# Weight sums of three FFN column blocks made during the softmax stage, and a reordered end of the down stage, in a hybrid decoder layer

## The chip, the cores and the metric

The kernel runs on one core of a Trainium2 chip. That core has five engines that work through their own instruction lists in order and wait for each other on semaphores: PE (TensorE, matrix products), DVE (VectorE), ACT (ScalarE), POOL (GpSimd) and SP (SyncE, which issues all DMAs here). The metric is the time of one execution on the device in microseconds (us).

## The reference

One decoder layer on a sequence of 1024 rows of width 1024, all in fp32. The middle (attention) is left out here; the parts that the change touches are the feed-forward network (FFN) and the last LayerNorm.

```python
mod = (c @ w_c + b_c).reshape(B, 6, D)              # shift, scale, gate for mixer and FFN
u = x * (1.0 + scale_m) + shift_m
proj = u @ w_in                                     # split into FoX and GLA parts
y = concat([fox_attention(...), gla_attention(...)]) @ w_o   # softmax heads, gated linear attention
x = layer_norm(ALPHA * x + (1.0 + gate_m) * y, ln1_g, ln1_b)
u2 = x * (1.0 + scale_f) + shift_f
h = silu(u2 @ w_gate) * (u2 @ w_up)                 # D_FF = 2816
y2 = h @ w_down
x = layer_norm(ALPHA * x + (1.0 + gate_f) * y2, ln2_g, ln2_b)
```

## The kernel before, in words

Every fp32 operand of a product is split into a high and a low part (`split`: a cast on ACT, L87, and a subtraction on DVE, L88), and each product is three matmuls (high x high, high x low, low x high). A matmul writes 128 rows x 512 columns of a PSUM bank. A scheduler decides the order of each engine's list when the kernel is built, from the order of the code and a few `after` and `issue_after` marks.

The program passes through these stages: modulation and projections, gated linear attention, the softmax heads (about 378 to 570 us of the profile below), the mixer's output with the first LayerNorm (to about 606), the FFN loop (to about 1050) and the down stage (to the end).

**The softmax heads.** Sixteen steps, four for each of four pairs of heads. `fox_load` brings the q and k rows of the next pair into four tiles named `stk` (loads of k_d and q_d, L748), in two column ranges. These tiles are the ones that the last scores of the pair before read, so their loads wait for these scores. `fox_scores` makes scores `sc` (PE, L766 and L767), an exponential (DVE L771, ACT L775, DVE L778, POOL L779, tile `pr`), and `fox_values` transposes `pr` (PE `tr`, L795) and multiplies with the values (PE `pv`, L807). Rows of the output projection (`yg`, `xbuf`, `rp_d`) fill in between.

**The FFN loop.** D_FF is cut into 22 column blocks of 128. For each, the gate and the up product of 1024 rows are made as one 2x2 block product with seven products in place of eight (Winograd's form). It needs sums of weights and sums of activations: `sum_weights(f, g, u, w)` splits B22 (the second half of up), makes T1 to T4 in place with four DVE operations (L1014 to L1017), and splits both tiles into `hi` and `lo`. `first_weights` splits the gate block itself (B11, B21). The activation sums S1 to S4 and A22 are made once by `second_operands` (DVE L972 for the sums, L88 and L87 for the splits, tiles `s` and `a`). A block's products run in `group_parts`; `first()` is the order of block 0 (T3, T1, T4, T2, B22). Tiles of a weight kind (`wtile("raw" / "hi" / "lo")`) have three buffers each, so a fourth one waits until all readers of the first have run.

**The mixer units** before the loop (`late`, tiles `r`): 12 matmuls `yo` for each of two halves of 512 columns and four row groups, then DVE adds the bank to the row (L894), and statistics and normalization follow. A unit's bank comes free with that addition. Two banks are in turn.

**The sums for the down stage.** `w_sums(i)`, called 11 times inside the loop, makes sums of two row blocks of w_down in place (tiles `wd`) and stores them to DRAM (`t_d`, two stores of 512 KB); `h_sums` does so for the activations h (`a_d`).

**The down stage.** Again seven products, each of six groups of two pieces of 128 contraction rows (one piece in the last group); `group` loads one group of both sides and splits it; `mms` issues its matmuls `dn` (L1213) for the four row groups q. Three products end with the banks being read to `dc` and added to the result rows: `add_rows` (multiply by the gate L1230, add L1231, statistics), then `out_norm` (L1307: subtract the mean, times l2g; L1314 or ACT L1311 with POOL L1312: times the deviation, plus l2b; two stores of 512 columns each). The last product, a_cols(1, 1) with t_rows(1, 0), goes onto the banks `sa` of the product before it; groups 2 to 5 are kept in SBUF, and the matmuls then go row group by row group, so that each row group's normalization follows while the next is multiplied.

SP issues the DMAs in the order of its list. Eight semaphores go round: a DMA waits until the one that used its semaphore before has landed.

## Time and profile before

| | |
|---|---|
| median of 3 runs | 1282.32 us (1281.34 to 1286.94) |
| the profiled execution | 1279.93 us, of which the span of the trace is 1278.1 |
| granted TensorE clock | 0.989 of full speed, mean |
| busy PE / DVE / ACT / POOL | 1222.8 / 794.4 / 514.3 / 225.2 us |
| DMA | 209.65 MB, 164 GB/s over the span |

Busy is the time in which an engine had an instruction in work; the rest of the span it waited. The granted clock tells how fast TensorE was let run; at 1.00 it is on the higher of its two levels (2.4 GHz), and a stretch well below 1.00 holds time on the lower one (1.2 GHz).

### The profile page before, as it was taken

To read this page: it belongs to the slowest core of one execution; us is meant where nothing else is said; L and a number is where in the kernel's file an instruction comes from. 1 tells how busy PE (TensorE), PEld (TensorE's weight loads), DVE (VectorE), ACT (ScalarE), POOL (GpSimd) and SP (SyncE) were. 2 spreads that over 40 slices of the span, in tenths; PEclk is the share of its full clock that TensorE was granted. 3 is DMA by queue.
4 is the path that set the end of the run, shared out by engine and by line. 5 is a ranking of instruction groups with operands and counts; after the bars stand their busy time and mean duration, and the time that the engine had idled before them with its cause. 6 is when DMAs were issued, how large, how long until landed. Compare 5 with 4: busy or idle time off the path is not lost.

```text
span 1278.1 us, 16493 instructions
## 1 busy us (share of the span) xinstructions
PE 1222.8 (96%) x6177; PEld 991.8 (78%) x6177; DVE 794.4 (62%) x1180; ACT 514.3 (40%) x876; POOL 225.2 (18%) x204
## 2 busy tenths in 40 slices
PE   6999999999999999999889999999999999999986
PEld 4889997899777767667768888888888887887875
DVE  7656529631554434548875665765765668585697
ACT  3422346422354466664623333333332344344341
POOL 3500032420233324322000000000000024060014
PEclk9999999999999999999989999999999999999999
DMA  9865625311465446133363454444444358675561
GB/s 298 258 221 189 202 65 173 108 42 40 137 196 162 145 126 202 67 133 112 102 214 131 142 180 173 173 161 144 174 166 162 125 206 287 223 238 189 196 232 66
DMA packets 144442, 209.65 MB, mean 164 GB/s; under 512 B 8100, under 2 KB 90406, under 8 KB 144364
## 3 DMA queue, kind: packets, MB, share of 16 engines
q1 hardware_dynamic: 144364, 208.62, 49.7%
q8 instruction: 48, 0.79, 0.2%
q14 instruction: 30, 0.25, 0.1%
HBM read 153.65 MB, written 54.94 MB: 163 GB/s over the span
## 4 chain that ended last, share of the span: by engine, by line
PE 75%; DVE 8%; DMA 7%; ACT 3%; POOL 3%; issue 3%; SPq 1%; POOLq 0%; DVEq 0%; ACTq 0%
PE ga L1028 18%; PE dn L1213 15%; PE gc L1028 9%; PE pv L807 4%; PE gb L1028 4%; DMA wc<-in_w_c_dram 4%; PE tr L795 3%; PE acc L330 2%; PE acc L332 2%; PE acc L331 2%; PE sc L767 1%; PE sc L766 1%; PE at L516 1%; DVE lo L88 1%; PE yg L717 1%
## 5 line engine op out<-in xcount | busy, mean ns | idle before, releaser
L88 DVE TENSOR_TENSOR lo<-raw,hi 128x1024 fp32r<-128x1024 f32 (+1 forms) x112 | 150.2, 1342 | 98.9 <-ACT hi L87 94.7
L87 ACT CAST hi<-raw 128x1024 fp32r<-128x1024 f32 (+1 forms) x112 | 114.7, 1026 | 123.3 <-PE ga L1028 44.5
L1028 PE MATMUL ga<-s,hi 128*128 128x512 f32 x344 | 109.0, 397 | 7.8 <-ACT hi L87 7.0
L1213 PE MATMUL dn<-hi,ah 128*128 128x512 f32 x280 | 111.7, 400 | 4.0 <-DVE dc L1287 3.5
L1213 PE MATMUL dn<-lo,ah 128*128 128x512 f32 x280 | 111.4, 398 | 2.5 <-DVE lo L88 2.4
L1213 PE MATMUL dn<-hi,al 128*128 128x512 f32 x280 | 110.4, 396 | 0.0
L1246 POOL TENSOR_TENSOR r<-r,l1g 128x1024 f32<-128x1024 f32 x8 | 23.3, 2920 | 491.1 <-DMA r<-z_d 490.0
L330 PE MATMUL acc<-hi,uh 128*128 128x264 f32 (+1 forms) x384 | 108.7, 284 | 0.5 <-ACT m L531 0.5
L332 PE MATMUL acc<-hi,ul 128*128 128x264 f32 (+1 forms) x384 | 108.7, 284 | 0.0
L331 PE MATMUL acc<-lo,uh 128*128 128x264 f32 (+1 forms) x384 | 108.7, 283 | 0.0
L88 DVE TENSOR_TENSOR al<-ar,ah 128x1024 fp32r<-128x1024 f32 (+1 forms) x38 | 54.5, 1436 | 49.6 <-ACT ah L87 49.3
L1028 PEld LDWEIGHTS ga<-s,hi 128*128 128x128 f32 x344 | 65.6, 191 | 24.0 <-ACT hi L87 7.5
L87 ACT CAST ah<-ar 128x1024 fp32r<-128x1024 f32 (+1 forms) x38 | 37.3, 984 | 101.7 <-PE dn L1213 95.8
L771 DVE CUSTOM_DVE_ANT_0 pr<-sc,smask 128x128 f32<-128x128 f32 (+7 forms) x64 | 47.8, 756 | 44.1 <-PE tr L795 19.2
L330 PEld LDWEIGHTS acc<-hi,uh 128*128 128x128 f32 x384 | 72.8, 190 | 1.6 <-issue 0.8
L331 PEld LDWEIGHTS acc<-lo,uh 128*128 128x128 f32 x384 | 72.8, 190 | 0.6 <-issue 0.2
L332 PEld LDWEIGHTS acc<-hi,ul 128*128 128x128 f32 x384 | 72.7, 190 | 0.4 <-issue 0.2
L1028 PE MATMUL ga<-s,lo 128*128 128x512 f32 x172 | 68.7, 400 | 0.0
L1213 PEld LDWEIGHTS dn<-hi,ah 128*128 128x128 f32 x280 | 53.4, 191 | 17.2 <-issue 3.9
L779 POOL TENSOR_SCALAR pr<-pr,sm 128x128 f32<-128x128 f32 (+7 forms) x64 | 48.5, 762 | 98.6 <-DVE sm L778 74.8
L1213 PEld LDWEIGHTS dn<-lo,ah 128*128 128x128 f32 x280 | 53.3, 190 | 15.4 <-DVE lo L88 3.3
L801 ACT COPY pt<-tr 128x512 f32<-128x512 f32 (+1 forms) x80 | 43.0, 542 | 53.3 <-PE tr L795 52.2
(347 smaller groups left out, 2924.0 us busy)
## 6 DMA issues: line engine op xcount, KB each, us to landing
ar<-a_d SPq DMA_DIRECT2D x35, 512.0 KB
wc<-in_w_c_dram SPq DMA_DIRECT2D x32, 512.0 KB
raw<-in_w_gate_dram SPq DMA_DIRECT2D x25, 512.0 KB
wd<-in_w_down_dram SPq DMA_DIRECT2D x22, 512.0 KB
t_d<-wd SPq DMA_DIRECT2D x22, 512.0 KB
a_d<-hf SPq DMA_DIRECT2D x22, 512.0 KB
u<-in_w_up_dram SPq DMA_DIRECT2D x21, 512.0 KB
raw<-t_d SPq DMA_DIRECT2D x20, 512.0 KB
```

The lines of the kernel that those rows point to most:

```text
L87: nc.scalar.copy(dst_hi, src)
L88: return nc.vector.tensor_tensor(dst_lo, src, dst_hi.bitcast(F32), op=ALU.subtract).ins
L330: nc.tensor.matmul(ps, uh[k][:, ts], wh[:, k % 4, :], start=k == 0, stop=False)
L331: nc.tensor.matmul(ps, uh[k][:, ts], wl[:, k % 4, :], start=False, stop=False)
L332: nc.tensor.matmul(ps, ul[k][:, ts], wh[:, k % 4, :], start=False, stop=k == NK - 1)
L771: nc.vector.tensor_tensor_reduce(t[:, 0:nk], sc[:, 0:nk], smask[:, S - nk : S], op0=ALU.add, op1=ALU.min, scale=-1.0, scalar=3e38, accum_o ...
L779: nc.gpsimd.tensor_scalar(t[:, 0:nk], t[:, 0:nk], sm[:, 2:3], 1.0, op0=ALU.mult, op1=ALU.mult)
L795: nc.tensor.transpose(tr[:, m * P : (m + 1) * P], ps_[2 * j + par][:, (2 * kk + a) * P : (2 * kk + a + 1) * P], ident,)
L801: nc.scalar.copy(pt[:, par, 0:w], tr[:, 0:w])
L807: nc.tensor.matmul(pv[64 * par : 64 * par + 64, q0:256], fv_t(kb)[:, 64 * h : 64 * h + 64], pt[:, par, a * 256 : a * 256 + 256 - q0], star ...
L1028: ins = nc.tensor.matmul(ps, x, y, start=start and j == 0 and i == 0, stop=j == NJ - 1 and i == 2, skip_group_check=not start,)
L1213: last["dn"] = nc.tensor.matmul(ps, x[:, a, qs], y[:, a, :], start=start and a == 0 and i == 0, stop=stop and a == n - 1 and i == 2, skip_ ...
```

## The change

Three things change, and two small ones with them. (1) For blocks 0, 1 and 2 of the FFN the sums T1 to T4 and B22 are made during the softmax heads (`pre_sums`, in the order 1, 2, 0; 9 pieces over the first seven steps, by the table `PRE`) and stored, already split, to DRAM: five tiles of 512 KB per block, `p_d`. At the FFN's start `load_sums` loads them, and `sum_weights` is no longer called for these blocks. (2) `w_sums` also splits its T4 part and stores the two parts (`t4_d`). The last product of the down stage loads them in place of loading and splitting. (3) At the end of the down stage the reads of the four banks come ahead of the fourth `out_norm` of the first half and of the `add_rows` of the second, and row group 3 is multiplied in two column ranges of 256. The last normalization of row group 2 moves from ACT and POOL to DVE, behind that of row group 3.

```diff
+    def pre_sums(f):
+        def load():
+            for n, i, src in (("g", 28, w_gate), ("u", 29, w_up)):
+                t = s_[n] = slot(i, (NK, P), name="pw")
+                nc.sync.dma_start(t, src[:, f * P : (f + 1) * P].rearrange("(k p) n -> p k n", p=P))
+        def sums():
+            b = slot(30, (2, NJ, P), dt=F32R, name="pb")
+            split(b[:, 0], b[:, 1], u[:, NJ:NK])
+            nc.sync.dma_start(p_d[f][0], b.rearrange("p a k n -> p (a k n)").bitcast(F32))
+            weight_sums(g, u)
+        def parts():
+            for k, (n, t) in enumerate((
+                ("u", slot(31, (NK, P), dt=F32R, name="ph")),
+                ("g", cp.tile([P, NK, P], F32R, tag="c4a", name=nm("ph"))),
+            )):
+                raw = s_[n]
+                split(t, raw.bitcast(F32R), raw)
+                nc.sync.dma_start(p_d[f][1 + 2 * k], t.rearrange("p k n -> p (k n)").bitcast(F32))
+                nc.sync.dma_start(p_d[f][2 + 2 * k], raw.rearrange("p k n -> p (k n)"))
+        return [load, sums, parts]
...
-    def load_up(f):
-        u = wtile("raw", (NK, P), F32) if f == 0 else slot((4, 5)[f % 2], (NK, P), name="u")
+        u = slot((4, 5)[f % 2], (NK, P), name="u")
...
+    def load_sums(f, w):
+        t14 = wtile("hi", (NK, P), F32R), wtile("lo", (NK, P), F32R)
+        if f == 1:
+            t32 = [slot(i, (NK, P), dt=F32R, name="t32") for i in (4, 5)]
+        else:
+            t32 = wtile("hi", (NK, P), F32R), wtile("lo", (NK, P), F32R)
+        b = slot((3, 25)[f % 2], (2, NJ, P), dt=F32R, name="b22")
+        for k, t in ((1, t32[0]), (2, t32[1]), (3, t14[0]), (4, t14[1])):
+            nc.sync.dma_start(t.rearrange("p k n -> p (k n)").bitcast(F32), p_d[f][k])
+        nc.sync.dma_start(b.rearrange("p a k n -> p (a k n)").bitcast(F32), p_d[f][0])
...
     def w_sums(i):
...
-        for k, w in enumerate((w0, w1)):
-            nc.sync.dma_start(t_d[i // 2][i % 2, k, :, :], w.rearrange("p a n -> p (a n)"))
+        t4h = cp.tile([P, 512], F32R, tag="m1", name=nm("t4h"))
+        t4l = w1[:, 0, :].bitcast(F32R)
+        split(t4h, t4l, w1[:, 0, :])
+        nc.sync.dma_start(t_d[i // 2][i % 2, 0, :, :], w0.rearrange("p a n -> p (a n)"))
+        nc.sync.dma_start(t_d[i // 2][i % 2, 1, :, 512:1024], w1[:, 1, :])
+        nc.sync.dma_start(t4_d[i // 2][i % 2, 0, :, :], t4h.bitcast(F32))
+        nc.sync.dma_start(t4_d[i // 2][i % 2, 1, :, :], w1[:, 0, :])
...
             split(ah, al, raw)
-            split(bh, bl, braw)
+            if bsrc is not None:
+                split(bh, bl, braw)
+            else:
+                for k, t in enumerate((bh, bl)):
+                    nc.sync.dma_start(t.bitcast(F32), t4_d[m][0:n, k, :, :].rearrange("i p n -> p i n"))
...
-            out_norm(0, q, ra[q], bsa[q], l2g, l2b)
+            if q < 3:
+                out_norm(0, q, ra[q], bsa[q], l2g, l2b)
         product(sa, a_cols(2, 1), t_rows(0, 1), False)
...
         for q in range(4):
-            nc.vector.tensor_tensor(c5[q], sa[q], c5[q], op=ALU.add)
-            add_rows(rb, bsb, q, 1, c5[q])
-        asrc, bsrc = a_cols(1, 1), t_rows(1, 0)
+            c22 = nc.vector.tensor_tensor(c5[q], sa[q], c5[q], op=ALU.add).ins
+        asrc = a_cols(1, 1)
         for m in range(2):
-            g = group(m, asrc, bsrc)
+            g = group(m, asrc, None)
             for q in range(4):
                 mms(sa[q], q, g, False, False, False)
-        kept = [group(m, asrc, bsrc, True) for m in range(2, NG)]
+        with tc.issue_after(c22):
+            out_norm(0, 3, ra[3], bsa[3], l2g, l2b)
+            kept = [group(m, asrc, None, True) for m in range(2, NG)]
+            for q in range(4):
+                add_rows(rb, bsb, q, 1, c5[q])
         for q in range(4):
-            for g in kept:
-                mms(sa[q], q, g, False, g is kept[-1], False)
             t = slot(30, (512,), name="tmp") if q % 2 else tmpb
...
+            for cs in (slice(0, 512),) if q < 3 else (slice(0, 256), slice(256, 512)):
+                for g in kept:
+                    mms(sa[q], q, g, False, g is kept[-1], False, cs)
+                nc.vector.tensor_tensor(t[:, cs], sa[q][:, cs], gf[:, cs], op=ALU.mult)
+                nc.vector.tensor_tensor(rb[q][:, cs], rb[q][:, cs], t[:, cs], op=ALU.add)
...
+            if q != 2:
+                end = out_norm(1, q, rb[q], bsb[q], l2g, l2b)
+            else:
+                m2 = first_norm(rb[q], bsb[q], l2g)[0]
+        with tc.issue_after(end):
+            last_norm(1, 2, rb[2], m2, l2b)
...
+    PRE = (1, 2, 1, 1, 2, 1, 1) + (0,) * 9
...
+        for _ in range(PRE[idx]):
+            pre.pop(0)()
...
-    g = load_gate(0)
-    sum_weights(0, g, load_up(0), ws[0])
+    load_sums(0, ws[0])
```

Three places in the lists show how the instructions move (line numbers are those of the file in question; a trailing number tells tiles of one name apart).

SP, in the softmax stage, at the loads of the second pair of heads. Before:

```order
167 L700 DMA rp_d<-xbuf 128x512
168 L694 DMA xbuf<-in_x_dram 128x512
169 L700 DMA rp_d<-xbuf 128x512
170 L694 DMA xbuf<-in_x_dram 128x512
171 L748 DMA stk_3058<-k_d_1800 128x256
172 L748 DMA stk_3060<-k_d_1800 66x256
173 L748 DMA stk_3057<-q_d_1796 128x768
174 L748 DMA stk_3058<-k_d_1800 128x768
```

And now, with `pw` the raw gate and up blocks and `p_d` the stored sums:

```order
172 L843 DMA p_d_3_3065<-ph_3663 128x1024
173 L844 DMA p_d_2_3064<-pw_3557 128x1024
174 L694 DMA xbuf<-in_x_dram 128x512
175 L844 DMA p_d_4_3066<-pw_3555 128x1024
176 L700 DMA rp_d<-xbuf 128x512
177 L827 DMA pw_3769<-in_w_up_dram 128x8x128
178 L827 DMA pw_3767<-in_w_gate_dram 128x8x128
179 L694 DMA xbuf<-in_x_dram 128x512
180 L748 DMA stk_3073<-k_d_1800 128x256
181 L748 DMA stk_3075<-k_d_1800 66x256
182 L748 DMA stk_3072<-q_d_1796 128x768
183 L748 DMA stk_3073<-k_d_1800 128x768
```

The loads `stk` stand behind stores of sums and loads of the next block's weights, where before only rows of the output projection stood.

PE, in block 0 of the FFN, from T2 (tile `s` 971 to 974 before, 983 to 986 now, is S2) to the next block's first product. Before:

```order
3014 L1028 MATMUL ga_5633<-s_972_5808,hi_5549 128x512 x2
3015 L1028 MATMUL ga_5633<-s_972_5808,lo_5550 128x512
3016 L1028 MATMUL ga_5633<-s_973_5811,hi_5549 128x512 x2
3017 L1028 MATMUL ga_5633<-s_973_5811,lo_5550 128x512
3018 L1028 MATMUL ga_5633<-s_974_5814,hi_5549 128x512 x2
3019 L1028 MATMUL ga_5633<-s_974_5814,lo_5550 128x512
3020 L1028 MATMUL gc_5848<-s_975_5821,b_928_5542 128x512 x3
3021 L1028 MATMUL gc_5848<-s_976_5824,b_928_5542 128x512 x3
3022 L1028 MATMUL gc_5848<-s_977_5827,b_928_5542 128x512 x3
3023 L1028 MATMUL gc_5848<-s_978_5830,b_928_5542 128x512 x3
3024 L1028 MATMUL ga_5676<-s_971_5805,hi_5919 128x512 x2
```

And now (`hi_5627` and `lo_5628` are block 0's T3 and T2, `hi_6070` and `lo_6071` are block 2's):

```order
3009 L1079 MATMUL gc_5924<-s_978_5862,lo_5626 128x512
3010 L1079 MATMUL ga_5709<-s_983_5881,hi_5627 128x512 x2
3011 L1079 MATMUL ga_5709<-s_983_5881,lo_5628 128x512
3012 L1079 MATMUL ga_5709<-s_984_5884,hi_5627 128x512 x2
3013 L1079 MATMUL ga_5709<-s_984_5884,lo_5628 128x512
3014 L1079 MATMUL ga_5709<-s_985_5887,hi_5627 128x512
3015 L1079 MATMUL ga_5807<-s_983_5881,hi_6070 128x512 x2
3016 L1079 MATMUL ga_5709<-s_985_5887,hi_5627 128x512
3017 L1079 MATMUL ga_5709<-s_985_5887,lo_5628 128x512
3018 L1079 MATMUL ga_5709<-s_986_5890,hi_5627 128x512 x2
3019 L1079 MATMUL ga_5709<-s_986_5890,lo_5628 128x512
3020 L1079 MATMUL ga_5807<-s_983_5881,lo_6071 128x512
```

The first matmuls with block 2's T2 have moved into block 0's T2. The loads of `hi_6070` and `lo_6071` go into the buffers of `hi_5625` and `lo_5626`, and so wait for the last matmuls with these (the first row here and the one before it).

DVE, at the end of the down stage (`dn` 8610 to 8613 before, 8725 to 8728 now, are the four banks `sa`). Before:

```order
1075 L88 TENSOR_TENSOR al_9999<-ar_9994,ah_9998 128x1024
1076 L1314 SCALAR_TENSOR_TENSOR r_1352_8810<-r_1352_8810,mv_9748,l2b_9256 128x512 x2
1077 L88 TENSOR_TENSOR kp_10071<-ar_10066,kp_10070 128x1024
1078 L88 TENSOR_TENSOR lo_10001<-raw_9996,hi_10000 128x1024
1079 L1314 SCALAR_TENSOR_TENSOR r_1367_8880<-r_1367_8880,mv_9761,l2b_9256 128x512 x2
1080 L88 TENSOR_TENSOR kp_10073<-raw_10068,kp_10072 128x1024
1081 L1287 TENSOR_TENSOR dc_9508<-dn_8610,dc_9508 128x512
1082 L88 TENSOR_TENSOR al_10035<-ar_10030,ah_10034 128x1024
1083 L1287 TENSOR_TENSOR dc_9508<-dn_8611,dc_9508 128x512
1084 L88 TENSOR_TENSOR lo_10037<-raw_10032,hi_10036 128x1024
1085 L1287 TENSOR_TENSOR dc_9509<-dn_8612,dc_9509 128x512
1086 L1287 TENSOR_TENSOR dc_9509<-dn_8613,dc_9509 128x512
```

And now:

```order
1080 L1387 SCALAR_TENSOR_TENSOR r_1372_8925<-r_1372_8925,mv_9863,l2g_9297 128x1024
1081 L1397 SCALAR_TENSOR_TENSOR r_1358_8845<-r_1358_8845,mv_9837,l2b_9371 128x512 x2
1082 L1397 SCALAR_TENSOR_TENSOR r_1365_8885<-r_1365_8885,mv_9850,l2b_9371 128x512 x2
1083 L88 TENSOR_TENSOR al_10091<-ar_10088,ah_10090 128x1024
1084 L1397 SCALAR_TENSOR_TENSOR r_1372_8925<-r_1372_8925,mv_9863,l2b_9371 128x512 x2
1085 L1355 TENSOR_TENSOR dc_9623<-dn_8725,dc_9623 128x512
1086 L88 TENSOR_TENSOR al_10125<-ar_10122,ah_10124 128x1024
1087 L1355 TENSOR_TENSOR dc_9623<-dn_8726,dc_9623 128x512
1088 L1355 TENSOR_TENSOR dc_9624<-dn_8727,dc_9624 128x512
1089 L1355 TENSOR_TENSOR dc_9624<-dn_8728,dc_9624 128x512
```

The four splits `kp` and `lo` that stood ahead of or between the bank reads, and the normalization of `r_1367` ahead of them, are gone from this stretch. That row's normalization comes later.

## Rows read from the trace of the kernel before

**Rows 1.** Page, part 1: busy us (share of the span) x instructions.

```profile
PE 1222.8 (96%) x6177; PEld 991.8 (78%) x6177; DVE 794.4 (62%) x1180; ACT 514.3 (40%) x876; POOL 225.2 (18%) x204
```

**Rows 2.** Busy by stretch: length, PE, PEld, DVE, ACT, POOL (count), clock, DMA, GB/s.

```profile
400.00:420.00 20.00, 20.00 (x115) 14.69 (x114) 9.69 (x25) 10.92 (x24) 4.44 (x6) 1.00 0.73 210
420.00:440.00 20.00, 20.00 (x108) 13.82 (x107) 5.61 (x17) 6.85 (x16) 8.06 (x9) 1.00 0.48 161
...
630.00:650.00 20.00, 10.57 (x35) 7.18 (x34) 19.34 (x30) 7.23 (x10) 0.00 (x0) 0.74 0.20 59
...
1240.00:1268.00 28.00, 28.00 (x123) 22.66 (x121) 25.13 (x36) 5.30 (x7) 9.66 (x7) 1.00 0.14 53
```

**Rows 3.** PE's waits, whole span: for whom, us in total, times, longest.

```profile
PE ga L1028 <- ACT hi L87: 7.0, 1, 7.0
...
PE dn L1213 <- DVE dc L1287: 3.5, 1, 3.5
...
PE yo L891 <- DVE r L894: 2.9, 1, 2.9
...
PE gc L1028 <- ACT hi L87: 1.2, 1, 1.2
```

**Rows 4.** Timeline of PE, mixer units: start, us, instruction, count, idle before.

```profile
590.53 0.64 PE L891 MATMUL yo<-wo,ofh 128*128 128x512 f32 x1 [2.90 <-DVE r L894]
...
593.96 0.49 PE L893 MATMUL yo<-wo,ofl 128*128 128x512 f32 x1
594.28 0.39 PE L891 MATMUL yo<-wo,ofh 128*128 128x512 f32 x1
```

**Rows 5.** Timeline of DVE, same place.

```profile
589.19 0.69 DVE L1014 TENSOR_TENSOR raw<-raw,raw 128x512 f32<-128x512 f32 x1 [3.02 <-DMA raw<-in_w_up_dram]
```

**Rows 6.** Timeline of PE, start of the FFN loop.

```profile
633.46 2.97 PE L1028 MATMUL gc<-s,b 128*128 128x512 f32 x12 [0.48 <-DVE hf L1133]
643.46 1.22 PE L1028 MATMUL ga<-s,hi 128*128 128x512 f32 x2 [7.03 <-ACT hi L87]
```

**Rows 7.** Timeline of DVE, the weight sums of blocks 1 and 2.

```profile
635.03 0.69 DVE L88 TENSOR_TENSOR b<-u,b 128x512 fp32r<-128x512 f32 x1
...
645.25 1.22 DVE L88 TENSOR_TENSOR lo<-u,hi 128x1024 fp32r<-128x1024 f32 x1
```

**Rows 8.** Timelines of SP and ACT: a 512 KB load's issue and its first reader.

```profile
614.42 0.38 SPq L997 DMA_DIRECT2D u<-in_w_up_dram  x1
...
618.44 0.62 ACT L87 CAST b<-u 128x512 fp32r<-128x512 f32 x1 [0.27 <-DMA u<-in_w_up_dram]
```

**Rows 9.** Timeline of DVE, end of the down stage.

```profile
1220.43 1.27 DVE L1307 SCALAR_TENSOR_TENSOR r<-r,mv,l2g 128x1024 f32<-128x1024 f32 x1
...
1225.40 2.73 DVE L1314 SCALAR_TENSOR_TENSOR r<-r,mv,l2b 128x512 f32<-128x512 f32 x4
1228.05 1.22 DVE L88 TENSOR_TENSOR al<-ar,ah 128x1024 fp32r<-128x1024 f32 x1
...
1235.24 0.68 DVE L1287 TENSOR_TENSOR dc<-dn,dc 128x512 f32<-128x512 f32 x1
```

**Rows 10.** Timeline of PE, same place.

```profile
1236.07 0.76 PE L1213 MATMUL dn<-hi,ah 128*128 128x512 f32 x1 [3.53 <-DVE dc L1287]
...
1238.76 0.86 PE L1213 MATMUL dn<-hi,ah 128*128 128x512 f32 x2
```

**Rows 11.** Timelines of DVE and POOL, the last row group.

```profile
1268.36 0.69 DVE L1299 TENSOR_TENSOR tmp<-dn,gf 128x512 f32<-128x512 f32 x1
...
1270.86 2.35 DVE L1307 SCALAR_TENSOR_TENSOR r<-r,mv,l2g 128x1024 f32<-128x1024 f32 x1
1273.65 1.42 DVE L1314 SCALAR_TENSOR_TENSOR r<-r,mv,l2b 128x512 f32<-128x512 f32 x2 [0.44 <-POOL mv L850]
...
1269.64 2.48 POOL L1312 TENSOR_TENSOR r<-r,l2b 128x512 f32<-128x512 f32 x2 [0.83 <-ACT r L1311]
```

**Rows 12.** Timelines of SP and PE, second pair of heads.

```profile
399.74 0.75 SPq L748 DMA_DIRECT2D stk<-k_d  x2
...
404.12 0.30 PE L766 MATMUL sc<-stk,stk 128*128 128x128 f32 x1
```

**Rows 13.** POOL by line, 378 to 570: busy us, mean ns, idle before, releasers.

```profile
L779 POOL TENSOR_SCALAR pr<-pr,sm 128x512 f32<-128x512 f32 (+7 forms) x58 | 44.7, 774 | 93.7 <-DVE sm L778 69.9 <-PE tr L795 13.5 <-PE sc L766 9.2
```

More of the change, by code (lines that the diff above doesn't have):

```diff
@@ L815, in fox_values, with weight_sums @@
         split(ofh[hp][:, qs], ofl[hp][:, qs], pv[:, 0:256])
+    p_d = [[dp.tile([P, 1024], F32, name=f"p_d{f}_{k}") for k in range(5)] for f in range(3)]
+    def pre_sums(f):
+        NJ = NK // 2
+        s_ = {}
+        def load():
[3 more added lines that the diff above has]
+        def sums():
+            g, u = s_["g"], s_["u"]
+            b = slot(30, (2, NJ, P), dt=F32R, name="pb")
[12 more added lines that the diff above has]
+        return [load, sums, parts]
+    def weight_sums(g, u):
+        lo_, hi_ = slice(0, NK // 2), slice(NK // 2, NK)
+        nc.vector.tensor_tensor(g[:, lo_], u[:, lo_], g[:, lo_], op=ALU.subtract)
+        nc.vector.tensor_tensor(u[:, lo_], u[:, hi_], u[:, lo_], op=ALU.subtract)
+        nc.vector.tensor_tensor(u[:, hi_], u[:, hi_], g[:, lo_], op=ALU.subtract)
+        nc.vector.tensor_tensor(g[:, hi_], g[:, hi_], u[:, hi_], op=ALU.subtract)
     ofh, ofl = [], []
@@ L979, in stage @@
                     put(ops, name, S_HL[j][i], out(j))
-        stage("S3", 0, a11, "t", a11, a21, ALU.subtract)
+        stage("S3", 0, a11, None, a11, a21, ALU.subtract)
         stage("S1", 1, a21, "sum", a21, a22, ALU.add)
@@ L1039, in hymba_layer_kernel @@
     t_d = [dp.tile([2, 2, P, D], F32, name=f"t_d{m}") for m in range(NG)]
+    t4_d = [dp.tile([2, 2, P, 512], F32, name=f"t4_d{m}") for m in range(NG)]
     hs_ = {}
@@ L1202, in group, with mms @@
             split(ah, al, raw)
-            split(bh, bl, braw)
+            if bsrc is not None:
+                split(bh, bl, braw)
+            else:
+                for k, t in enumerate((bh, bl)):
+                    nc.sync.dma_start(t.bitcast(F32), t4_d[m][0:n, k, :, :].rearrange("i p n -> p i n"))
             pc[0] += 1
             return n, ah, al, bh, bl
-        def mms(ps, q, g, start, stop, new):
+        def mms(ps, q, g, start, stop, new, cs=slice(0, 512)):
             n, ah, al, bh, bl = g
@@ L1213, in mms @@
                     last["dn"] = nc.tensor.matmul(
-                        ps, x[:, a, qs], y[:, a, :], start=start and a == 0 and i == 0,
+                        ps[:, cs], x[:, a, qs], y[:, a, cs], start=start and a == 0 and i == 0,
                         stop=stop and a == n - 1 and i == 2, skip_group_check=not new,
@@ L1308, in out_norm @@
         for h in range(2):
             hs = slice(h * 512, (h + 1) * 512)
-            if half == 1 and q < 3:
+            if half == 1 and q < 2:
                 nc.scalar.mul(r[:, hs], r[:, hs], mv[:, 2:3])
@@ L1317, in out_norm @@
             nc.sync.dma_start(outr[t * P : (t + 1) * P, hs], r[:, hs])
+    def out_norm(half, q, r, bs, l2g, l2b):
+        mv, ins = first_norm(r, bs, l2g)
+        last_norm(half, q, r, mv, l2b)
+        return ins
     fills = [(h, t) for h in range(2) for t in range(NT)]
@@ L1325, in hymba_layer_kernel @@
     late = []
+    pre = [f for b in (1, 2, 0) for f in pre_sums(b)]
+    PRE = (1, 2, 1, 1, 2, 1, 1) + (0,) * 9
     for idx, (hp, i) in enumerate(steps):
@@ L1393, in hymba_layer_kernel @@
             p1()
-        if f > 0:
-            with after("lo" if f < 3 else None):
-                with after("u" if f == 2 else None):
-                    u = load_up(f)
-                sum_weights(f, g, u, w)
-        if f >= 3:
+            sum_weights(f, g, load_up(f), w)
             p2()
```

38 lines of the change are left out of this document (21 added, 17 removed).

## The prediction

> **What bounds the kernel now.** The first view is the page's busy times: PE works 96% of the span, the next engine 62% [rows 1]. So only a PE wait, or work behind PE's last matmul, can give time back, and work moved between the other engines is free where PE stays fed. The second view is busy time by stretch. PE is busy throughout in the softmax stretches and most of the way to the end; from 630 to 650 it is busy only 10.57 of 20 us, at a mean clock of 0.74, while DVE is busy 19.34 [rows 2]. The third is the list of PE's waits: 7.0 us and 1.2 us for ACT's `hi`, 2.9 us for DVE's `r`, 3.5 us for DVE's `dc` [rows 3]. The change touches the places of all four.
>
> Each of the three places must be read with what follows it. After the wait of 2.90 us, nine matmuls from 590.53 to 594.28 take 3.75 us [rows 4]; twelve at full clock take 2.97 us with the latency of the last [rows 6], some 0.23 us each, so nine should take 2.1. The low clock after the wait costs another 1.7 us. After the 3.53 us wait six matmuls take 2.69 us, 1.3 more than at 0.23 [rows 10].
>
> **FFN start, the mixer units.** At 589.19 DVE begins the first sum of block 0 (L1014), having stood 3.02 us for the up weights' DMA [rows 5]. The addition that frees PE's bank stands behind it in DVE's list. With the loads of sums this L1014 is gone from DVE's list; the wait of 2.90 and the slow matmuls (1.7) make 4.6 us. Not all of it: in the new list the split of block 2's gate tile (DVE 1.2 us, ACT 1.05 us, durations as in rows 7 for a 1024 split) stands ahead of the same addition, and its load is issued late. I put 0.9 us against it, with 0 and 2.6 as bounds (not late at all; landing 0.3 us sooner than the up weights did, and no low clock). **Gain 3.7 us (2.0 to 4.6).**
>
> **FFN start, the sums of blocks 1 and 2.** DVE makes these from 635.03 on [rows 7], with the finishing work of block 0 between, and PE waits 7.03 us to 643.46 for the first split part [rows 6], then 1.2 [rows 3], then runs some eight matmuls at the low clock; by the 1.7 of [rows 4] that is 1.7 us again, so 9.9 us in all. These sums are gone. What is late next? The activation sums S and A22 still run on DVE, as before; PE's short waits for them (0.48 in [rows 6]) stay. And the lists show a new wait: `hi_6070` and `lo_6071` (block 2's T3 and T2) may only be loaded when PE has done the last matmuls with block 0's T1, and the first matmul with them stands seven matmuls later, 1.6 us. A 512 KB load takes 4.0 us from issue to its reader [rows 8]. So PE waits 4.0 - 1.6 = 2.4 us; part may be covered if PE waits there for S2 anyway. I take 2.2 us. The waits of 2.9 and 3.5 us were followed by the low clock and that of 0.5 not, so 0 to 1.7 us for that, taken as 1.0. The other new loads have more cover (`hi_5986` is released by the last A12 product of block 2, some 70 matmuls or 16 us ahead of its use). 9.9 - 2.2 - 1.0 = 6.7 us. **Gain 6.7 us**, from 5 (load at 5 us, full low clock, some 1 us for `lo` behind `hi`) to 9.5 (no wait).
>
> The Trainium skill, "DMA: Bandwidth & Descriptors", section "Anatomy of one DMA", gives 2.0 us fixed plus bytes by 436 GB/s; for 512 KB that is an estimate of 3.2 us, against 4.0 in [rows 8]. By it the wait would be 1.6 us and the whole forecast 0.6 lower; I keep the trace's 4.0.
>
> **Down stage, bank reads.** DVE works without a break from 1220.43 (first L1307) to 1235.24 (first bank read) [rows 9], while PE has been done since 1232.5 (1236.07 less 3.53, [rows 10]). The new order has, from the same start, three L1307 (1.26 each, 3.8), six L1314 (2.73 for four, so 4.0) and one split `al` (1.2) ahead of the read: 9.0 us, so DVE is there at 1229.4, before PE has finished its last group. Reads of later banks follow at 0.6 each with one split between, done by 1233.7; PE needs the second bank only six matmuls after the first. So the wait of 3.53 and the 1.3 us of low clock go [rows 10]. New on this path are the loads of T4's parts, which go into buffers released by the groups before; the first has the 36 matmuls of two later groups (8.4 us) as cover against 4.0 for a load [rows 8], two at once perhaps 5.5. The second pair stands in SP's list behind four output stores that wait for L1314 of rows 0 and 1, done by 1227, and is needed 24 matmuls after the first. **Gain 4.8 us (3 to 5.2).** The work that is put off (fourth `out_norm`, four `add_rows`, kept splits) needs about 14 us of DVE from 1233.7, where the old list had five more splits; PE works 16 us until the first row group is done, so it stays hidden. If it did not, the first evacuation would be late, but PE's other three banks go on.
>
> **The tail.** Before, PE's last matmul ends just ahead of 1268.36; then DVE takes two operations and statistics of 0.69, L1307 in 2.35 us (beside POOL's L1312), a wait for POOL and L1314 in 1.42: to 1275.07, 6.7 us [rows 11]. After: row group 2's L1307 (1.27) stands in DVE's list ahead of the last half's evacuation and holds it some 0.9 us past PE's end; then three operations of half width (about 0.43 each), statistics (0.3), L1307 at 1.27 [rows 9] since no L1312 runs beside it, and four L1314, two of them for row group 2, at 2.73 [rows 9]. That is 0.9 + 1.3 + 0.3 + 1.2 + 2.7 = 6.4. The halved row group gains, the second row group on DVE gives it back. **Gain 0.3 us (-1 to 1.5).**
>
> **Softmax stage.** Added per block: five DVE operations of 512 columns (0.6 to 0.69) and two splits of 1.2, some 5.9 us, 17.7 for three; ACT 8; DMA 21 transfers of 512 KB, 10.5 MB. DVE is busy 9.7 and 5.6 of 20 us there and DMA 0.73 and 0.48 [rows 2], so both have room. Not free is the order: in SP's list the loads of the second pair of heads now stand behind four stores that wait for splits, and behind two weight loads that wait for these stores to land. Before, they were issued at 399.74, and PE's first score with them came at 404.12 without a wait [rows 12], about a load's 4.0 us later. So what delays the issue can reach PE directly, unless output projection work fills. **Loss 1.5 us**: 0 if the stores land before 399.7, 5 if each of the two pairs behind such stores is 2.5 us late (a landing of 4.0 less some cover).
>
> **Free.** The T4 split in `w_sums` (11 times 0.69 on DVE, 0.62 on ACT) falls where PE is busy throughout and DVE is not; were the cover gone, 7 us. The split stores carry 0.25 MB more per call, 11 calls in the 400 us of the loop.
>
> **Sum.** 3.7 + 6.7 + 4.8 + 0.3 - 1.5 = 14.0 us from the profiled 1279.9: 1265.9. The median of the runs is 2.4 above the profiled execution, so 1282.3 - 14.0 = **1268.3**, say 1268.
>
> **Rivals.** Half a per cent, 6.4 us, is about what a measurement of this kernel can tell from none: faster is below 1275.9, slower above 1288.7.
>
> *The wait moves into DMA (0.18).* The loads of block 2's sums, and its gate tile, come later than I say: both terms at their lower bounds, 2.0 + 5 in place of 10.4. For it: SP's list is in order and a semaphore of eight is shared. Against: SP is nearly idle at 614 [rows 8]. 1268.3 + 3.4 = 1271.7.
>
> *The softmax stage pays (0.15).* Both late pairs cost 2.5 us each and the 21 DVE operations on the way hold back `pr`, 0.6 to 1.2 us where one stands ahead of a score's exponential: some 5 of 21 at 1 us. The loss is 10 in place of 1.5: 1276.8, no change. For it: PE has no idle time to absorb it [rows 2]. Against: POOL stands 93.7 us idle in this stage, and `pr` waits there [rows 13].
>
> *DVE's sums block POOL (0.05).* L1307 took 1.27 alone and 2.35 beside L1312 [rows 9, 11], so two such operations do not run side by side. The new sums and splits, 17.7 us, could each hold up `pr` (44.7 us of POOL [rows 13]) or be held up by it. If a third of them is seen by PE, that is 6 us more: 1274. The Trainium skill, "SBUF — State Buffer", section "Who interferes with whom", has this as an exclusive lock for DVE operations with two SBUF inputs; rows 9 and 11 agree with it.
>
> *Slower (0.04).* The stores to `p_d` hold SP's in-order list so that the loads of all three later pairs of heads come late. Each load then must wait for a landing and PE stands. It decides when the three together cost more than 14.0 + 1.5 + 6.4 = 22 us, over 7 us each; at 8 each the time is 1282.3 - 15.5 + 24 = 1290.8. The 2.4 us by which I assume a pair to be late speak against it.
>
> *No change for other reasons (0.03)*, 1280: the loop's own order shifts and gives the time back.
>
> The forecast itself has 0.55, from 1263 to 1272. Its bounds and the first two rivals give **1262 to 1277**. Faster 0.55 + 0.18 + 0.05 and 0.04 of the second rival, whose cost is spread about 10 us, 0.82; same its other 0.11 and 0.03, 0.14; slower 0.04.
>
> **What will show it.** DVE without L1014 to L1017 between 585 and 650, PE without a wait for `r`; the wait of 7.0 replaced by one of 2 us on a DMA `hi<-p_d`; no wait of PE for `dc`; the first matmul of the last product at once behind the last of the one before; from PE's last matmul to DVE's last operation still 6 to 7 us. In the softmax stage, `stk` loads no more than 3 us later against the scores. Wrong would be a new PE wait on a `stk` load, on `tr`, or on T4's parts, or a wait of over 4 us at block 2's sums.

## The result, and the profile after

The changed kernel takes 1269.68 us (median of 4 runs, 1267.35 to 1272.4), the one before 1281.83 beside it: a ratio of 0.9898 (95% interval 0.9876 to 0.992), 12 us faster where 14 were forecast. The first profiled execution is the slowest of the four, 1272.4 us with a span of 1270.4; a second profile, from the repeat below, has a span of 1265.4. In some executions the part ahead of the softmax stage ran at a lower granted clock and took longer (16 to 35 us in the profiles of start_only, end_only, gate2_late, t4_raw and tail_q2_pool, of which only stretches from the first score on are read); ratios leave such executions out, medians and ranges hold them.

The page's busy times barely move against [rows 1], and the stretches show where they did.

```profile
PE 1221.7 (96%) x6198; PEld 989.8 (78%) x6198; DVE 796.4 (63%) x1191; ACT 513.8 (40%) x879; POOL 232.4 (18%) x202
```

Busy time by stretch of the changed kernel (columns as in [rows 2]):

```profile
400.00:420.00 20.00, 20.00 (x116) 14.20 (x115) 15.30 (x32) 13.87 (x27) 5.13 (x6) 1.00 0.98 319
420.00:440.00 20.00, 19.87 (x109) 13.89 (x109) 12.16 (x29) 10.60 (x24) 10.57 (x10) 1.00 0.83 278
630.00:650.00 20.00, 18.46 (x80) 14.50 (x79) 12.99 (x22) 7.76 (x14) 0.00 (x0) 1.00 0.46 157
```

From 400 to 440 DVE, ACT and DMA carry the new sums while PE stays full. From 630 to 650 PE works 18.46 us in place of 10.57, at full clock in place of 0.74. PE's waits of the changed kernel, those at the places of the change:

```profile
PE dn L1276 <- DVE lo L88: 4.2, 4, 1.5
...
PE tr L795 <- POOL pr L779: 2.4, 1, 2.4
PE yo L930 <- DVE r L933: 2.0, 1, 2.0
...
PE sc L767 <- DMA stk<-k_d: 1.4, 1, 1.4
PE ga L1079 <- DMA hi<-p_d: 1.3, 1, 1.3
PE dn L1276 <- DMA hi<-t_d: 1.2, 1, 1.2
```

Of [rows 3], the waits of 7.0, 3.5 and 1.2 us are gone. In place of the 7.0 stands 1.3 for block 2's parts, in place of the 3.5 stands 1.2 for T4's. The wait for `r` is still there, 2.0 after 2.9. New too is a wait of 1.4 for `stk`.

Where the time came from is read between the same PE instructions in both timelines: the second half of the first score (L767; 348.15 before, 346.12 and 345.74 in the two profiles after; "first score" from here on), the first `u2p` (569.25; 572.01, 568.21), the last `yo` (600.20; 603.17, 599.42), the first `gc<-s` (623.01; 625.77, 621.99), the last `ga<-a1h` (1024.79; 1018.80, 1015.32), the short wait for ACT's `dc` in the down stage (1171.19; 1166.22, 1161.24), PE's last matmul's end (1268.33; 1260.48, 1255.48), the span's end. The differences, in us:

| stretch | before | after, 1st | after, 2nd | gain, 1st and 2nd | forecast |
|---|---|---|---|---|---|
| softmax stage, to the first u2p | 221.10 | 225.89 | 222.47 | -4.8, -1.4 | -1.5 |
| mixer units, to the last yo | 30.95 | 31.16 | 31.21 | -0.2, -0.3 | 3.7 |
| to the first gc<-s | 22.81 | 22.60 | 22.57 | 0.2, 0.2 | 0 |
| FFN loop, to the last ga<-a1h | 401.78 | 393.03 | 393.33 | 8.75, 8.45 | 6.7 |
| down stage, to the wait for dc | 146.40 | 147.42 | 145.92 | -1.0, 0.5 | 0 |
| its end, to PE's last matmul | 97.14 | 94.26 | 94.24 | 2.9, 2.9 | 4.8 |
| tail | 9.77 | 9.92 | 9.92 | -0.15, -0.15 | 0.3 |

With the 2.0 and 2.4 us by which the first score came sooner, in a part that the change does not touch, these are the 7.7 and 12.7 us between the spans. Of those, some 1.7 us are clock (an estimate: length times what is missing from the clock): the profile before has a wait of 2.09 us there with a granted clock of 0.74 and 0.83 behind it (128 to 136 us), and both profiles after are at 1.00. The down stage's start, with no edit that was forecast to matter there, moves by a us either way; PE's waits for DVE's `lo` are 2.4 us in all before, 4.2 and 3.4 after, and what sets them was not tried.

**Mixer units.** The wait of 2.03 us and nine matmuls of 0.63, at the low clock, as in [rows 4]. Timeline of PE in the changed kernel:

```profile
596.23 0.56 PE L930 MATMUL yo<-wo,ofh 128*128 128x512 f32 x1 [2.03 <-DVE r L933]
...
599.58 0.57 PE L932 MATMUL yo<-wo,ofl 128*128 128x512 f32 x1
599.98 0.40 PE L930 MATMUL yo<-wo,ofh 128*128 128x512 f32 x1
```

What stands ahead of that `r` addition is no longer L1014 of [rows 5] but the split of block 2's gate tile. Timelines of SP, ACT and DVE, same place:

```profile
587.20 0.37 SPq L1031 DMA_DIRECT2D raw<-in_w_gate_dram  x1
...
591.55 1.05 ACT L87 CAST hi<-raw 128x1024 fp32r<-128x1024 f32 x1 [2.61 <-PE yo L932]
...
592.63 1.22 DVE L88 TENSOR_TENSOR lo<-raw,hi 128x1024 fp32r<-128x1024 f32 x1 [2.04 <-ACT hi L87]
...
594.38 1.21 DVE L88 TENSOR_TENSOR a1l<-af,a1h 128x1024 fp32r<-128x1024 f32 x1
595.50 1.28 DVE L933 TENSOR_TENSOR r<-r,yo 128x512 f32<-128x512 f32 x2
```

The load is issued at 587.20, read by ACT 4.35 us later; DVE stands 2.04 us for the cast, and a split of 1.22, statistics and a split of 1.21 come before the addition. The cast's row names PE; in the second profile the same cast, 4.48 us after the issue, waits for the load by name.

These two profiles are not the whole picture. Five more (start_only, t4_raw, t4_whole, tail_q2_pool, pre_b) have the gate split at the same place and a wait for `r` of 1.73 to 2.05 us, but a clock of 1.00 behind it, and the units take 28.98 to 29.46 us: a gain of 1.5 to 2.0 in place of -0.2.

**Sums.** `hi<-p_d` is issued at 631.74 and PE goes on at 635.37, after 1.33 us and at full clock. SP itself waits for PE before that issue (its waits from 629 to 640 us).

```profile
631.74 0.32 SPq L1068 DMA_DIRECT2D hi<-p_d  x1
...
635.37 0.93 PE L1079 MATMUL ga<-s,hi 128*128 128x512 f32 x3 [1.33 <-DMA hi<-p_d]
...
SPq L1068 <- PE gc L1079: 7.7, 1, 7.7
```

**Bank reads.** Timelines of DVE, SP and PE, and SP's waits from 1222.3 to 1225.6 us:

```profile
1225.48 0.69 DVE L1355 TENSOR_TENSOR dc<-dn,dc 128x512 f32<-128x512 f32 x1 [1.21 <-PE dn L1276]
...
1225.04 0.41 SPq L1266 DMA_DIRECT2D hi<-t_d  x1
...
1231.52 0.47 PE L1276 MATMUL dn<-hi,ah 128*128 128x512 f32 x1 [1.17 <-DMA hi<-t_d]
...
SPq L1266 <- PE dn L1276: 3.0, 2, 2.5
```

DVE now waits for PE ahead of the first bank read, as forecast; PE's new wait is for the second pair of T4's parts, issued 6.5 us ahead of its reader. The four output stores ahead of it in SP's list were issued by 1222.2; what SP then waits for is PE.

### The profile page after: what moved, and what is told of

The parts are those of the page before. It is cut to its first block, busy times and chain, and to the rows that moved or that the text cites. A ratio compares the mean times of both kernels' runs of the same rounds, so it can differ in the third digit from the quotient of the medians.

```text
span 1270.4 us, 16681 instructions
## 1 busy us (share of the span) xinstructions
PE 1221.7 (96%) x6198; PEld 989.8 (78%) x6198; DVE 796.4 (63%) x1191; ACT 513.8 (40%) x879; POOL 232.4 (18%) x202
## 4 chain that ended last, share of the span: by engine, by line
PE 73%; DMA 10%; DVE 9%; issue 3%; ACT 2%; POOL 1%; SPq 1%; DVEq 0%; ACTq 0%; POOLq 0%
PE ga L1079 17%; PE dn L1276 14%; PE gc L1079 9%; DMA wc<-in_w_c_dram 5%; PE pv L807 4%; PE gb L1079 4%; PE tr L795 3%; PE acc L330 2%; PE acc L332 2%; PE acc L331 2%; DVE lo L88 2%; PE sc L766 1%; PE at L516 1%; DMA wd<-in_w_down_dram 1%; PE sc L767 1%
## 5 line engine op out<-in xcount | busy, mean ns | idle before, releaser
L88 DVE TENSOR_TENSOR lo<-raw,hi 128x1024 fp32r<-128x1024 f32 (+1 forms) x106 | 143.1, 1351 | 101.3 <-ACT hi L87 86.0
L87 ACT CAST hi<-raw 128x1024 fp32r<-128x1024 f32 (+1 forms) x106 | 108.5, 1024 | 115.7 <-PE ga L1079 40.3
L1079 PE MATMUL ga<-s,hi 128*128 128x512 f32 x328 | 103.6, 396 | 1.5 <-DMA hi<-p_d 1.3
L1079 PEld LDWEIGHTS ga<-s,hi 128*128 128x128 f32 x328 | 61.7, 188 | 17.3 <-issue 1.7
L779 POOL TENSOR_SCALAR pr<-pr,sm 128x128 f32<-128x128 f32 (+7 forms) x64 | 53.8, 845 | 105.5 <-DVE sm L778 91.0
L1079 PE MATMUL ga<-s,lo 128*128 128x512 f32 x164 | 65.0, 397 | 0.3 <-DVE lo L88 0.3
L1079 PE MATMUL gc<-s,b 128*128 128x512 f32 x264 | 63.6, 390 | 0.0
```

The lines of the kernel that those rows point to most:

```text
L87: nc.scalar.copy(dst_hi, src)
L88: return nc.vector.tensor_tensor(dst_lo, src, dst_hi.bitcast(F32), op=ALU.subtract).ins
L779: nc.gpsimd.tensor_scalar(t[:, 0:nk], t[:, 0:nk], sm[:, 2:3], 1.0, op0=ALU.mult, op1=ALU.mult)
L1079: ins = nc.tensor.matmul(ps, x, y, start=start and j == 0 and i == 0, stop=j == NJ - 1 and i == 2, skip_group_check=not start,)
```

## The experiments

Eight edits, in ten kernels and twelve runs, each beside runs of the kernel before on the same chip. Ratios are to that kernel, with the 95% interval. `tail_q2_pool`, `t4_whole` and `pre_b` ran once each and are read from their profiles alone.

**The whole change again, its two halves, and the gate split moved.** `after_again` is the changed kernel; `start_only` has `pre_sums` and `load_sums` with the old `w_sums` and down stage; `end_only` has T4's parts and the new end of the down stage with the old start. In `gate2_late` cast and split of block 2's gate tile stand behind the last `a1h` cast and the last `r` addition (the lines that set these two marks are left out here):

```
...
-    first_weights(load_gate(2), ws[2])
+    with after("a1"), after("radd"):
+        first_weights(load_gate(2), ws[2])
```

> The changed kernel once more, unaltered, for a second profiled execution. The forecast's own terms (theory A) give 14 us below the kernel before. The first trace, read term by term (theory B), gives about 6 us from the change (8.7 at the block sums, 2.9 at the bank reads, less 4.8 in the softmax stage and 1 at the start of the down stage) and 2 us from a stage that the change does not touch. Theory B expects the same waits in the second trace: one of about 2 us for DVE's r with slow matmuls behind it near 596, two of stk loads near 455 with slow matmuls behind them, and one of about 1 us for T4's parts near 1231. If these are chance, they are gone or much shorter.

> Only the weight sums in the softmax stage and their loads; the sums for the down stage and its end as before. Theory A (terms 3.7 + 6.7 - 1.5): about 9 us below the kernel before. Theory B (8.7 less 4.8 in the softmax stage, nothing at the mixer units): about 4 us.

> Only the T4 parts stored in the loop and the new end of the down stage; the softmax stage and the start of the FFN as before. Theory A (4.8 + 0.3): about 5 us below the kernel before. Theory B (2.9 less 0.2 at the tail): 2 to 3 us, with a wait of 1 us for T4's parts inside the last product.

> The changed kernel with one thing moved: the cast and the split of block 2's gate tile go behind the last cast of the mixer operands on ACT and the last addition of the mixer units on DVE. Theory B: the wait of 2.0 us for r and the nine slow matmuls (1.6 us) behind it go, 3.6 us less than the changed kernel. The forecast's reading (theory A, 0.9 us lost there): about 1 us less. A rival: the wait only moves, since the split then stands ahead of the last statistics and the rows for the second operands come 1.2 us later: no change.

| kernel | median us | ratio | interval |
|---|---|---|---|
| kernel before | 1282.70 | 1 | |
| after_again | 1267.74 | 0.9896 | 0.9877 to 0.9916 |
| start_only | 1273.92 | 0.9933 | 0.9912 to 0.9953 |
| end_only | 1281.59 | 0.9976 | 0.9959 to 0.9992 |
| gate2_late | 1277.62 | 0.9911 | 0.988 to 0.9943 |

The ratios make the start worth 8.6 us (1282.7 x 0.0067), the end 3.1, the whole 13.3. The interval for the end, 1.0 to 5.3 us, does not exclude the forecast's 5.1; its trace does better: from the wait for `dc` to the span's end `end_only` takes 104.49 us against 106.91, 2.4 less, with the same new wait for T4's parts, 1.4 us, with the old start. `gate2_late` had no wait for `r` in its trace and 27.16 us in the mixer units, but its times scatter too far to tell 4 us of total.

**Again, with T4's second pair in other buffers, and the tail as before.** `gate2_again` is `gate2_late`. `t4_raw` loads the second group's parts into the free `raw` buffers; `gate2_t4` has both edits. `tail_q2_pool` gives row group 2's last operations back to ACT and POOL and keeps the halves of row group 3.

```
-                bh, bl = wtile("hi", (n, 512), F32R), wtile("lo", (n, 512), F32R)
+                kinds = ("raw", "raw") if bsrc is None and m == 1 else ("hi", "lo")
+                bh, bl = [wtile(k, (n, 512), F32R) for k in kinds]
```

> The changed kernel with the cast and split of block 2's gate tile behind the last r addition, once more, since the first timing was spread. Theory A (that split is what keeps PE waiting 2 us for r, and the low clock after it costs as much again): no wait for r, 27 us from the first u2p to the last yo in place of 31, nothing late later, so 4 us less than the changed kernel: about 1264, ratio to before 0.986. Theory B (the stage gets shorter, but the gate tile is then late for its first product and gives it back): the total stays at that of the changed kernel, 1268, ratio 0.989 to 0.990, and PE has a new wait of 2 us or more for a part of block 2.

> The changed kernel with the second group's -T4 parts loaded into the free raw buffers in place of hi and lo, so that no release by an earlier group stands before these loads. Theory A (the wait of 1.2 us for hi<-t_d is the release of the buffers): the wait goes or falls under 0.3, and the bank reads then gain 4 of the forecast 4.8; total 1.2 us less than the changed kernel, ratio 0.9885. Theory B (the loads are late because they stand behind output stores in SP's list): the wait stays at 1.0 to 1.3, the total is unchanged, 0.9896.

> Both edits together. Theory A: 4 + 1.2 us less than the changed kernel, about 1262.5, ratio 0.985. Theory B: neither or only one helps, 1264 to 1268, ratio 0.986 to 0.990.

> The changed kernel with row group 2's last operations on ACT and POOL, as before the change; the halves of row group 3 stay. Theory A (as forecast: the halves gain some 1.3 us and row group 2 on DVE gives it back): DVE's last operation ends 1.3 us sooner behind PE's last matmul, and the span from PE's last matmul to the end falls from 10.0 to about 8.7. Theory B (POOL's two additions of row group 2 hold up the mean and variance of row group 3, which POOL finishes, or end last themselves): 10 to 12 us, no better.

`gate2_again` 1267.14 us, ratio 0.9871 (0.9844 to 0.9898); `t4_raw` 0.9865 (0.9834 to 0.9897); `gate2_t4` 0.9891 (0.9851 to 0.9931). The totals cannot tell these steps apart; the traces can. PE by stretch in the changed kernel and then in `gate2_again` (start and end, length, PE busy and count, granted clock, DMA share, GB/s):

```profile
590.00:595.00 5.00, 4.16 (x17) 1.00 0.91 352
595.00:600.00 5.00, 3.77 (x10) 0.66 0.01 5
```

```profile
590.00:595.00 5.00, 5.00 (x24) 1.00 0.65 258
595.00:600.00 5.00, 5.00 (x24) 1.00 0.54 213
```

The mixer units take 27.23 us here and 27.36 in `gate2_t4`, with no wait for `r`. Against 31.16 and 31.21 that is theory A's 4 us, against the five profiles with the wait but without the low clock 1.6 to 2.2. Theory B's new wait of 2 us did not come: PE's wait for block 2's parts is 1.48, after 1.33 and 1.21, and the FFN loop takes 393.72, after 393.03 and 393.33. That its span is no shorter than the second one of the changed kernel (1265.6 and 1265.4) lies in other stretches: its softmax stage is 2.3 us longer, with a wait of 2.0 for `stk` at the fourth pair of heads, and the down stage up to the wait for `dc` 1.1 us.

In `t4_raw` and `gate2_t4` no wait for T4's parts is left (theory A). That alone does not part the theories, as the edit also brings these loads ahead of the output stores in SP's list; but SP's own wait for PE in the changed kernel, 3.0 us with the stores already issued, is the release of `hi` and `lo` by earlier groups. From the wait for `dc` to the span's end it is 101.7 us in both, 104.2 in both profiles of the changed kernel, so 2.5 us rather than 1.2. The other 1.3 lies in what follows, and its cause is argued, not tried by itself: the scheduler also built another order of PE's last matmuls. In the changed kernel those of row groups 0 and 1 alternate, so that DVE reads them at 1248.37 and 1249.76; in `t4_raw` they are read 3.7 us apart, and the first one 3.7 us sooner after the wait for `dc`.

`tail_q2_pool` goes theory B's way: 11.52 us from PE's end to the span's, 9.92 with row group 2 on DVE. Timelines of POOL and DVE:

```profile
1292.53 3.24 POOL L1390 TENSOR_TENSOR r<-r,l2b 128x512 f32<-128x512 f32 x2 [0.83 <-ACT r L1389]
1295.73 0.54 POOL L889 TENSOR_TENSOR mv<-mv,half_neg 128x1 f32<-128x1 f32 x1
...
1296.31 1.42 DVE L1392 SCALAR_TENSOR_TENSOR r<-r,mv,l2b 128x512 f32<-128x512 f32 x2 [2.88 <-POOL mv L889]
```

POOL makes row group 3's scale (L889) only when it is done with row group 2's additions; DVE stands 2.88 us for it.

**Block 2's parts, the halves, the sums' place.** `all3` is `gate2_t4` with T3 and T2 of block 2 in `raw` buffers as well; `t4_whole` is `t4_raw` with row group 3 read in one piece; `pre_b` was to move the nine pieces of the sums to steps 4, 5 and 6 of the softmax loop. The edits of the three, one after the other (`t4_whole`'s with the lines for the statistics left out):

```
-            t32 = wtile("hi", (NK, P), F32R), wtile("lo", (NK, P), F32R)
+            t32 = [wtile("raw" if f == 2 else k, (NK, P), F32R) for k in ("hi", "lo")]
...
-            for cs in (slice(0, 512),) if q < 3 else (slice(0, 256), slice(256, 512)):
+            for cs in (slice(0, 512),):
...
-    PRE = (1, 2, 1, 1, 2, 1, 1) + (0,) * 9
+    PRE = (0, 0, 0, 0, 3, 3, 3) + (0,) * 9
```

> The changed kernel with three edits: block 2's gate split behind the last r addition, the second group's -T4 parts in raw buffers, and block 2's T3 and T2 parts in raw buffers too, so that their loads need not wait until PE is done with block 0's T1. Theory A (the prediction's step: the 1.2 to 1.5 us wait for hi<-p_d at block 2's sums is the release of hi and lo): that wait goes or falls under 0.3, and the block sums gain 9.5 to 10 of the forecast's 9.9 in all; total 4 + 1.6 + 0.9 + 1.3 us less than the changed kernel, 1260, ratio 0.983 to 0.985. Theory B (the parts are late for another reason, SP's list or the stores to p_d): the wait stays at 1.2 or more, total 1261.5 to 1264.

> The changed kernel with the second group's -T4 parts in raw buffers and row group 3 read in one piece of 512 columns in place of two halves; row group 2's last operations stay on DVE. With halves the span from PE's last matmul's end to the span's end is 9.0 us, and PE waits 0.5 us for DVE's read of the first half. Theory A (the prediction: halves take 1.3 us off the tail): 10.2 to 10.5 us here, PE's last matmul ends 0.5 sooner, so halves gain 0.8 net. Theory B (the halves gain nothing, the gain at the tail is row group 2 on DVE): 9.5 us here with PE ending 0.5 sooner, so the end of the span is the same.

> The changed kernel with the nine pieces of the three blocks' sums moved to the steps 4, 5 and 6 of the softmax loop (three each), so that all stores of parts stand shortly ahead of the third pair's loads. From the first score to the first u2p the stage takes 221.1 us before the change, 222.5 and 225.9 in two profiles of the changed kernel. Theory A (the stores and weight loads hold up the stk loads at the hand-over, as the prediction has it): PE's waits for stk at the third pair sum to 3 us or more, stage 227 or longer. Theory B (the waits of 0.7 to 1.9 us there are not set by the sums' transfers; the rest of the cost is PE's other order): 222 to 226 with stk waits of 0.5 to 2 us.

`all3`: 1261.38 us, ratio 0.984 (0.9787 to 0.9893; five of six runs 1259.77 to 1261.95, one 1277.87). Its trace has no wait for `p_d`, `t_d` or `r`, and the FFN loop takes 391.74 us, 1.3 to 1.6 less than in the changed kernel. With SP's wait for PE of 7.7 us ahead of this load in the changed kernel, that is theory A, the release of the buffers. Its stretch from 630 to 650:

```profile
630.00:650.00 20.00, 20.00 (x88) 16.37 (x88) 9.61 (x15) 5.53 (x9) 0.00 (x0) 1.00 0.40 114
```

`t4_whole`: from the wait for `dc` to the span's end 101.48 us without halves, 101.67 with them in `t4_raw`, one profile each (theory B: the halves gain nothing). What they cost shows in PE's timeline of `all3`, and what they were to save in DVE's of `t4_whole`:

```profile
1247.44 2.41 PE L1278 MATMUL dn<-kp,kp 128*128 128x256 f32 x18 [0.52 <-DVE tmp L1374]
```

```profile
1250.41 0.69 DVE L1373 TENSOR_TENSOR tmp<-dn,gf 128x512 f32<-128x512 f32 x1 [1.08 <-PE dn L1277]
1251.14 0.69 DVE L1374 TENSOR_TENSOR r<-r,tmp 128x512 f32<-128x512 f32 x1
1251.87 0.69 DVE L882 BATCH_NORM_STATS2 bs<-r 128x6 f32<-128x512 f32 x1
```

Both halves lie in one bank; in this program PE waits 0.52 us until DVE has read the first half before it writes the second, and it issues twice as many matmuls. The Trainium skill, "PSUM — Partial Sum Buffer", section "PSUM bank collisions raise a hardware error", says that two engines on one bank must be kept apart by bank and quadrant of 32 partitions, not by address, so that other columns do not help. The wait of 0.52 agrees with a program that does so.

`pre_b`: the stage takes 223.57 us, and the waits for `stk` sum to 0.75, as theory B has it. But the edit did not do what its text says. The scheduler decides the lists, and it built those of PE, ACT and POOL as before the edit, SP's with two `stk` loads in another place and DVE's with one reciprocal. The first store of sums is issued 36.9 us behind the first score in the changed kernel and 37.0 in `pre_b`, and the last one 7.3 us ahead of the third pair's loads in both (442.95 and 450.25; 445.55 and 452.85 in `pre_b`). So `pre_b` is one more profile of the changed kernel and parts neither theory.

**The three edits without the halves.**

> The three edits together (block 2's gate split late, -T4 parts and block 2's T3 and T2 parts in raw buffers), and row group 3 read in one piece of 512 columns. Theory A (the halves gain nothing): the time from the down stage's wait for dc near 1160 to the span's end is 101.5 us, as with halves (101.7), the total that of the three edits, 1260 to 1262, ratio 0.982 to 0.985. Theory B (the halves gain 0.8, and the one look without them was by chance): 102.5 us, total 1261 to 1263.

1263.85 us, ratio 0.9848 (0.9823 to 0.9872), and 101.54 us from the wait for `dc` to the end, 101.65 with halves in `all3`: theory A for the halves. This interval ends just below that of the repeat of the changed kernel (0.9877 to 0.9916), so these edits beat both kernels. `all3` and `all3_whole` are not told apart.

## Why the prediction came out as it did

The total held, 1268 forecast against 1269.68 and 1267.74. That is in part luck: the mixer units and the bank reads gave less than forecast, the sums more, the stage ahead of the first score gave 2.0 and 2.4 us that nobody forecast, and the errors cancelled. Two of the prediction's own signs of being wrong came too, new waits of PE for `stk` (0.3 to 1.4 us) and for T4's parts (1.2 us).

**Mixer units, forecast 3.7, measured -0.2 and -0.3, and 1.5 to 2.0 in five more profiles.** The step that failed is "I put 0.9 us against it, with 0 and 2.6 as bounds". The order lists had shown the right instruction ahead of the addition, but it was priced by its own length and a landing, not by the chain at its place: issue at 587.20, 4.35 us to ACT, the cast, the split, and another split behind it. That left a wait of 1.7 to 2.2 us, and in two of seven profiles the low clock behind it took 1.7 more; the forecast had counted all of that clock as gained and put the lower bound at a wait without it. `gate2_again`, which moves only this work, has neither (27.2 us).

**Sums, forecast 6.7, measured 8.75 and 8.45.** The mechanism was right, the new wait mis-sized: 1.3 us in place of 2.2 (the load took 3.6 us from issue to reader, not 4.0, and PE reached it 2.3 us after the issue, not 1.6), and no low clock behind it in place of 1.0. 9.9 - 1.3 = 8.6. That the wait is the release of the buffers shows in SP's wait for PE and in `all3`. The fit from which the prediction took its estimate of 3.2 us (the Trainium skill, "DMA: Bandwidth & Descriptors", section "Anatomy of one DMA") is one for DMAs that GpSimd issues; all loads here are issued by SP.

**Bank reads, forecast 4.8, measured 2.9.** The old wait and its low clock are gone as forecast. The step that failed is the cover of T4's second pair, "needed 24 matmuls after the first": it is issued only when `hi` and `lo` are released, takes 6.5 us to its reader where the forecast had "perhaps 5.5" for two at once, and PE waits 1.17 us; and PE's wait for DVE's read of the first half (0.67) was not seen. 4.8 - 1.2 - 0.7 = 2.9, though the fit is closer than the terms: this stretch gains 4.5 us in `t4_raw`, without the first wait, and 5.4 in `t4_whole`, without either.

**Tail, forecast 0.3, measured -0.15.** Near in sum, wrong in both parts. The halves gain nothing net (101.67 and 101.48), and row group 2 on DVE does not give a gain back: it makes 1.6 us (11.52 against 9.92), as POOL would hold row group 3's scale.

**Softmax stage, forecast -1.5, measured -1.4 and -4.8.** The size is luck; the step that failed is the reason, stores ahead of the `stk` loads in SP's list. The second pair's scores come without a wait, and the third pair's loads are issued from 450.25 on, as the last scores of the pair before end, 7.3 us after the last store of sums. In the first profile PE waits 0.47 and 1.38 us for `stk` at the third pair and then runs at a clock of 0.66 from 455 to 465; in the second 0.36 and 0.30, at full clock. In ten more profiles with the sums in this stage it takes 222.7 to 225.1 us, against 221.1 and 221.4 in the two without. So the cost is 1.3 us at least, and up to 4.8 in a single execution.

The traces show what most of it is. PE waits for POOL's `pr` some 36 us after the first score, before the change too. Timelines of PE, the kernel before and then the second profile of the changed one:

```profile
384.40 0.55 PE L795 MATMUL tr<-ident,pr 128*128 128x128 f32 x3 [2.50 <-POOL pr L779]
...
385.02 0.39 PE L716 MATMUL yg<-lo,ogh 128*128 128x512 f32 x1
```

```profile
381.82 0.55 PE L795 MATMUL tr<-ident,pr 128*128 128x128 f32 x3 [2.51 <-POOL pr L779]
...
382.54 0.63 PE L716 MATMUL yg<-lo,ogh 128*128 128x512 f32 x1
```

The wait is the same, but in the second profile the granted clock over the 4 us behind it is 0.57 in place of 1.00, which costs 1.7 us. Ten of the twelve profiles with sums have this low clock, neither of the two without (where the wait is 2.50 and 1.66 us); in the first profile it comes at 455 instead, and in `t4_whole`, which has none, the waits for `stk` sum to 3.2 us. Taken together, the stage less PE's idle time and less what the low clock cost (estimated as above, in steps of 5 us) is 216.6 to 217.6 us in all fourteen profiles, with sums or without. So the cost is mostly waits and clock; whether the sums bring the low clock on, with a wait of the same length, stays open.

**The rivals.** Part of the first, the wait moving into DMA, took place: at block 2's sums, where it cost less than the rival had it, and at the gate tile, where it cost that or more. The wait for T4's parts is of the same kind, but the rival did not name it. The second, at 10 us, did not; nor did the third, since PE's wait for `pr` is 2.4 us after 2.5 before.

## What to carry to other kernels

When a change takes the last waiter off an in-order list, price what then stands first by its whole chain from the load's issue, not by its own length; moving that one piece behind the urgent operation gave 1.6 to 4.0 us in that stage, though no total here shows it by itself. A load into a buffer that an earlier group still reads is issued at the release, so its cover counts from there; two free buffers of another kind took both new waits away. Splitting the last piece of work within one accumulation bank bought nothing here, as PE then waited for DVE's read of the first half. A gain read from one profile of a stretch can be off by the 1.7 us of one stretch at the low clock, so compare several profiles. And look at the lists after an edit: moving code that a scheduler orders may move nothing.
